# A diffusion layer on one core: probabilities transposed through DRAM, partial sums seeded in PSUM, Newton rounds on GpSimd

## The chip, the core and the metric

The kernel runs on one core of a Trainium2 chip. A core has TensorE (PE, which loads weights and streams the moving operand past them), VectorE (DVE), ScalarE (ACT), GpSimd (POOL), and SyncE (SP), whose queue issues the DMA transfers of this kernel. PE writes to PSUM, a small memory of eight banks of 512 float32 columns; DVE, ACT and PE read SBUF, the large one. Each engine works through its own list of instructions in order and waits on semaphores for the others. The metric is device time in microseconds (us), as the median of several executions.

## The reference, cut to what matters

One layer over 256 latent tokens and 256 context tokens of width 2048, all in float32.

```python
sh1, sc1, g1, sh2, sc2, g2 = ada_mods(c, w_ada, b_ada)             # modulation of the latents
qa, ka, va, qb, kb, vb = mixer_qkv(modulate(x, sh1, sc1), w_in, ...)   # B: per-head rms norm of q, k; rotary
qac, kac, vac, qbc, kbc, vbc = mixer_qkv(modulate(ctx, csh1, csc1), w_in, ...)
heads = concatenate([window_sink_attention(qa, ka, va, kac, vac, sink_logit),
                     global_attention(qb, kb, vb, kbc, vbc)], axis=-1)
x = layer_norm(DN_ALPHA * x + g1 * (heads @ w_out), ln1_g, ln1_b)
x = layer_norm(DN_ALPHA * x + g2 * swiglu(modulate(x, sh2, sc2), w_gate, w_up, w_down), ln2_g, ln2_b)
```

There are 16 query heads of 128, eight in group A (windowed, with a sink) and eight in group B (global), each group with two key heads. A query attends in one softmax to 256 latent and 256 context keys, so a row of scores has 512 entries. For the product of probabilities and values the probabilities must lie with the keys on the partitions, while the softmax has the queries there: that is the transpose of which this change speaks.

## The kernel before, in words

Every weight product is done as three float32r products of split operands (`mm3`, lines 268 to 271): high by high, low by high, high by low. So a weight tile is loaded by SP (a "raw" buffer of 1 MB), its high part is cast by ACT and its low part subtracted by DVE (lines 491 and 494 in the first part, 259 and 260 in the second), and only then can PE use it.

The first part, up to about 406 us, is recorded as steps and put in order by a planner, `Flow`. Each step has an engine, a cost in ns, the steps it waits for, and the buffers that it takes and gives; a step can ask for its result to count as ready earlier or later than its end. `Flow.forward` plays the steps against the clock with these costs and lags (the lag after a step on SP is 2000 ns), `Flow.backward` gives each its latest start, and the best of eight rounds is the order in which the instructions are issued. So the planner's costs decide the order on each engine, and nothing is reordered on the chip.

In that part the layer's input is modulated and the combined projection is accumulated over five groups of input columns (`GROUPS`, with 1, 1, 2, 4 and 8 tiles of 128): `flow_block` makes the products of a group for one block of 512 output columns, and after each group the sum in PSUM is added on DVE to `qacc` or `kvacc` in SBUF (line 679). `head_rms` computes the reciprocal root for the norms of group B's heads: squares on ACT, then a first guess and three Newton rounds on small tiles of DVE (lines 288 to 290, 720). `flow_keys` and `flow_queries` rotate, transpose and split keys and queries.

`flow_attend` does the attention in 16 pairs of heads (four head groups of four heads, two blocks of 128 queries). For a pair: scores on PE, the largest on DVE (L873), exponentials on ACT (L885), the reciprocal on DVE (L895), the weighting on ACT (L898); then, for each of the two heads, four transposes on PE into a PSUM bank (L903) and a copy to SBUF by ACT (L908, `gather`); then the product with the values on PE (L914), a cast on ACT (L921) and a subtraction on DVE (L925). Pools set how many can be under way: `b4` has 18 tiles of 4 KB a partition, `t2k` five of 2 KB, `wk` and `acc` four PSUM banks each.

`flow_out` makes the output projection. It is done in pieces over the four head groups: a first piece is copied to `outacc` by ACT (L1080); a later one is added on DVE (L1086); the last is then gated (L1089), joined with the residual (L1092, L1095) and measured for the layer norm (L1098). While the attention runs, SP also brings `w_out` and the rest of `w_ada`, of which DVE makes the gate's sums (L377).

The second part, from about 406 us on, is the feed-forward network, in an order set by its loops and not by `Flow`. It already transposes its hidden activations by way of DRAM: `squares` (DVE transposes 32 by 32 blocks, L1367), `put` (four DMAs, one for each 32 partitions, L1372) and `get` (one DMA back, L1377).

Of the kernel before, what the change touches and what calls it, by code (L numbers as in the profile page):

```python
# [22 lines left out]
P = 128  # L23
# [30 lines left out]
PUT, GET, PLACE = 6, 8, 9  # L54

# [139 lines left out]
def dit_layer(ctx: ExitStack, tc: tile.TileContext, x, c, cx, c_ctx, w_ada, b_ada, w_in, q_norm_g,  # L195
# [72 lines left out]
    def mm3(ps, xh, xl, w, first, last):  # L268
        nc.tensor.matmul(ps, lhsT=xh, rhs=w[0], start=first, stop=False)  # L269
        nc.tensor.matmul(ps, lhsT=xh, rhs=w[1], start=False, stop=False)  # L270
        nc.tensor.matmul(ps, lhsT=xl, rhs=w[0], start=False, stop=last)  # L271

    def rsqrt_steps(ss, n, done):
# [12 lines left out]
        def newton(i):  # L286
            y, t = st["y"], st["t"]
            nc.vector.scalar_tensor_tensor(t, y, -0.5, y, op0=ALU.mult, op1=ALU.mult)
            nc.vector.tensor_mul(t, t, ss())
            nc.vector.scalar_tensor_tensor(y, t, 1.5, y, op0=ALU.add, op1=ALU.mult)  # L290
            if i == 2:
                done(y)

        return [first] + [lambda i=i: newton(i) for i in range(3)]

    ea = ExitStack()
# [203 lines left out]

    def flow_products(hl, deps, ready, cols, ps, xs, first, last, prev):

        def fn():
            if first:
                ps.t = acc_bank()
            for i, (c, x) in enumerate(zip(cols, xs)):
                xh, xl = x()
                mm3(ps.t, xh, xl, (hl.hi[:, c : c + NB], hl.lo[:, c : c + NB]),
                    first and i == 0, last and i == len(cols) - 1)
# [3 lines left out]
        return F.add("PE", 681 * len(cols), fn, after, [ps] if first else [], list(hl.rooms))  # L513
# [132 lines left out]
    def flow_block(g, b, chunks):  # L646
# [7 lines left out]
        ends = {}  # L654
# [19 lines left out]
        for r in rows:  # L674
            dst = qacc[gi][r] if kvi is None else kvacc[kvi][r // 2][:, r % 2, :]

            def evac(dst=dst, ps=accs[r], r=r):
                if g > 0:
                    nc.vector.tensor_add(dst, dst, ps.t)
                elif r % 2 or b < 2:  # L680
                    nc.vector.tensor_copy(dst, ps.t)
                else:
                    nc.scalar.copy(dst, ps.t)

            eng = "ACT" if g == 0 and not (r % 2 or b < 2) else "DVE"
            evacs[b, r] = F.add(eng, 520 if eng == "ACT" else 710, evac, [ends[r], evacs.get((b, r))], give=[accs[r]])
# [19 lines left out]
    def head_rms(srcs, nh, after, scale=None):  # L706
# [10 lines left out]
        def done(y):  # L717
            if scale is not None:
                f = pa.tile([P, n], F32, tag="qsc", name="qsc", bufs=4)
                nc.vector.tensor_scalar_mul(f, y, scale)  # L720
# [4 lines left out]
        for i in range(len(srcs)):  # L725
            for h in range(nh):
                squares.append(F.add("ACT", 440, lambda i=i, h=h: square(i, h), [*after, *squares[:1]]))
        prev = squares
        for f in rsqrt_steps(lambda: st["ss"], n, done):
            prev = [F.add("DVE", 720, f, prev)]  # L730
# [18 lines left out]
    def flow_keys(w):  # L749
# [10 lines left out]
        for r in range(4):  # L760
# [34 lines left out]
            else:  # L795
                a = F.add("DVE", 1360 * (r < 2) + 800 * w, turn, [ev[r], root, tables], [rot] if r < 2 else [])
            a = F.add("PE", 210, flip, [a], [ps], [rot] if r < 2 else [])
            a = F.add("ACT", 300, cast, [a, *kT[w][1][:1]], rooms if r == 0 else [])
            b = F.add("DVE", 420, rest, [a], give=[ps])
# [4 lines left out]
    def flow_queries(gi):  # L804
# [8 lines left out]
        for t in range(NT):  # L813
# [25 lines left out]
            for i, ns in enumerate((420, 420, 710, 710)):  # L839
# [3 lines left out]
            a = F.add("ACT", 500, cast, [a, *(c for c, _ in qT[gi][1])], rooms if t == 0 else [])  # L843
            b = F.add("DVE", 710, rest, [a], give=[ps])
            qT[gi][1].append((a, b))

    def flow_attend(gi, at, each):
# [5 lines left out]
        for p in range(4):  # L853
# [4 lines left out]
            pT, o_ps = Buf("b4"), Buf("wk")  # L858
# [41 lines left out]
            def flip(i, probs=probs, ps=None):  # L900
                ps.t = wk_bank()
                for k in range(4):
                    nc.tensor.transpose(ps.t[:, k * P : (k + 1) * P], probs[i].t[:, k * P : (k + 1) * P], ident)  # L903

            def gather(i, pT=pT, ps=None):
                if i == 0:
                    pT.t = b4([P, 4, 2, P], F32, "pT")
                nc.scalar.copy(pT.t[:, :, i, :], ps.t.rearrange("p (k q) -> p k q", k=4))  # L908

            def values(pT=pT, o_ps=o_ps):  # L910
                o_ps.t = wk_bank()
                for k in range(4):
# [296 lines left out]
    at = TO  # L1209
# [410 lines left out]
```

## Time and profile before

| What | Value |
|---|---|
| Median of three runs | 1156.96 us (1155.35 to 1157.27) |
| The profiled execution's own time | 1156.38 us |
| Its span, from the first to the last instruction | 1154.6 us |
| Mean granted TensorE clock | 0.996 |
| HBM read, written | 295.68 MB, 7.86 MB |
| Wait of PE for `crow`, the longest of all | 3.0 us |
| End of the last matmul, start of the closing layer norm | 1133 us |

How to read the profile's rows: a group's row has the source line, the engine, the operation, the tiles (out<-in), the shape and the count, then the busy time in us, the mean ns of one, and behind the second bar the idle time of the engine just before the group, with what ended it. A row of the waits has the engine and line that waited, what it waited for, then total us, number and longest. A row of the windows has a stretch of the span, its length, each engine's busy time in it (with the count of instructions), the granted clock, the share of the DMA engines and GB/s. A row of the timeline or of the chain starts with the start in us and the duration.

### The profile page before, as it was taken

To read this page: it belongs to the slowest core of one execution; us is meant where nothing else is said; L and a number is where in the kernel's file an instruction comes from. 1 tells how busy PE (TensorE), PEld (TensorE's weight loads), DVE (VectorE), ACT (ScalarE), POOL (GpSimd) and SP (SyncE) were. 2 spreads that over 40 slices of the span, in tenths; PEclk is the share of its full clock that TensorE was granted. 3 is DMA by queue.
4 is the path that set the end of the run, shared out by engine and by line. 5 is a ranking of instruction groups with operands and counts; after the bars stand their busy time and mean duration, and the time that the engine had idled before them with its cause. 6 is when DMAs were issued, how large, how long until landed. Compare 5 with 4: busy or idle time off the path is not lost.

```text
span 1154.6 us, 14326 instructions
## 1 busy us (share of the span) xinstructions
PE 1135.0 (98%) x5475; PEld 919.1 (80%) x5475; DVE 830.9 (72%) x1078; ACT 540.2 (47%) x772; POOL 26.1 (2%) x44
## 2 busy tenths in 40 slices
PE   8999999999999999999999999999999999999995
PEld 8766588888888768888888888888888888888884
DVE  4763489988899988777666666776776787676556
ACT  3331442678776255544464444544544344433341
POOL 1000030000000001000000000000000000000000
PEclk9999999999999999999999999999999999999998
DMA  8999998624588578989967776677677988876641
GB/s 263 382 381 394 396 363 311 221 74 160 185 316 296 175 250 309 349 305 317 312 196 258 224 244 223 225 248 250 227 247 248 323 308 301 315 292 236 208 142 74
DMA packets 166557, 304.49 MB, mean 264 GB/s; under 512 B 7340, under 2 KB 33356, under 8 KB 164183
## 3 DMA queue, kind: packets, MB, share of 16 engines
q1 hardware_dynamic: 166488, 303.58, 75.7%
q8 instruction: 43, 0.70, 0.2%
q14 instruction: 26, 0.21, 0.1%
HBM read 295.68 MB, written 7.86 MB: 263 GB/s over the span
## 4 chain that ended last, share of the span: by engine, by line
PE 94%; DVE 2%; DMA 2%; ACT 1%; issue 0%; SPq 0%; DVEq 0%; ACTq 0%
PE acc L269 27%; PE acc L270 27%; PE acc L271 27%; PE wk L914 2%; PE wk L530 2%; PE acc L1124 1%; PE wk L903 1%; DMA raw<-in_w_in_dram 1%; PE wk L269 1%; PE wk L271 1%; PE wk L270 1%; PE wk L387 1%; PE wk L617 1%; DMA lgb<-in_ln_b_dram 1%; PE wk L967 0%
## 5 line engine op out<-in xcount | busy, mean ns | idle before, releaser
L260 DVE TENSOR_TENSOR lo<-raw,hi 128x1024 fp32r<-128x1024 f32 x258 | 312.5, 1220 | 182.8 <-ACT hi L259 179.3
L259 ACT CAST hi<-raw 128x1024 fp32r<-128x1024 f32 x258 | 271.2, 1055 | 353.4 <-PE acc L271 306.5
L269 PE MATMUL acc<-hi,u2h 128*128 128x512 f32 x704 | 274.6, 390 | 0.2 <-ACT u2h L1443 0.2
L270 PE MATMUL acc<-lo,u2h 128*128 128x512 f32 x704 | 274.0, 389 | 0.7 <-DVE lo L260 0.7
L271 PE MATMUL acc<-hi,u2l 128*128 128x512 f32 x704 | 274.1, 389 | 0.0
L269 PEld LDWEIGHTS acc<-hi,u2h 128*128 128x128 f32 x704 | 132.2, 188 | 28.2 <-ACT u2h L1443 1.1
L270 PEld LDWEIGHTS acc<-lo,u2h 128*128 128x128 f32 x704 | 132.2, 188 | 28.2 <-DVE lo L260 1.1
L271 PEld LDWEIGHTS acc<-hi,u2l 128*128 128x128 f32 x704 | 132.2, 188 | 28.2 <-DVE u2l L1444 0.6
L491 ACT CAST hi<-raw 128x1024 fp32r<-128x1024 f32 (+1 forms) x86 | 87.9, 1033 | 127.2 <-PE acc L271 64.4
L269 PE MATMUL acc<-hi,hTh 128*128 128x512 f32 x344 | 135.5, 394 | 0.0
L271 PE MATMUL acc<-hi,hTl 128*128 128x512 f32 x344 | 133.9, 389 | 0.0
L270 PE MATMUL acc<-lo,hTh 128*128 128x512 f32 x344 | 133.9, 389 | 0.0
L377 DVE SCALAR_TENSOR_TENSOR adav<-raw,cs,adav 128x512 f32<-128x512 f32 (+1 forms) x128 | 121.2, 947 | 9.1 <-DMA raw<-in_w_ada_dram 7.4
L494 DVE TENSOR_TENSOR lo<-raw,hi 128x1024 fp32r<-128x1024 f32 (+1 forms) x86 | 101.8, 1195 | 27.2 <-ACT hi L491 27.0
L269 PE MATMUL acc<-hi,uh 128*128 128x512 f32 x256 | 103.9, 406 | 0.1
L270 PE MATMUL acc<-lo,uh 128*128 128x512 f32 x256 | 100.3, 392 | 0.8 <-DVE lo L494 0.8
L271 PE MATMUL acc<-hi,ul 128*128 128x512 f32 x256 | 100.0, 391 | 0.0
L270 PEld LDWEIGHTS acc<-lo,hTh 128*128 128x128 f32 x344 | 64.6, 188 | 14.4 <-issue 1.0
L269 PEld LDWEIGHTS acc<-hi,hTh 128*128 128x128 f32 x344 | 64.6, 188 | 14.1 <-issue 1.0
L271 PEld LDWEIGHTS acc<-hi,hTl 128*128 128x128 f32 x344 | 64.6, 188 | 13.4
L269 PEld LDWEIGHTS acc<-hi,uh 128*128 128x128 f32 x256 | 48.1, 188 | 15.8 <-issue 5.2
L270 PEld LDWEIGHTS acc<-lo,uh 128*128 128x128 f32 x256 | 48.2, 188 | 10.5 <-DVE lo L494 1.8
(206 smaller groups left out, 1167.5 us busy)
## 6 DMA issues: line engine op xcount, KB each, us to landing
raw<-in_w_ada_dram SPq DMA_DIRECT2D x72, 1024.0 KB, 7.3
raw<-in_w_gate_dram SPq DMA_DIRECT2D x44, 1024.0 KB, 7.3
raw<-in_w_up_dram SPq DMA_DIRECT2D x44, 1024.0 KB, 7.3
raw<-in_w_down_dram SPq DMA_DIRECT2D x44, 1024.0 KB, 5.2
raw<-in_w_ada_dram SPq DMA_DIRECT2D x48, 512.0 KB, 4.5
raw<-in_w_in_dram SPq DMA_DIRECT2D x18, 1024.0 KB, 9.9
raw<-in_w_out_dram SPq DMA_DIRECT2D x16, 1024.0 KB, 5.0
raw<-in_w_in_dram SPq DMA_DIRECT2D x10, 512.0 KB, 6.9
```

What stands on the lines that cost most here:

```text
L259: nc.scalar.copy(hi[:, :n], raw[:, s : s + n])
L260: nc.vector.tensor_tensor(lo[:, :n], raw[:, s : s + n], hi[:, :n].bitcast(F32), op=ALU.subtract)
L269: nc.tensor.matmul(ps, lhsT=xh, rhs=w[0], start=first, stop=False)
L270: nc.tensor.matmul(ps, lhsT=xh, rhs=w[1], start=False, stop=False)
L271: nc.tensor.matmul(ps, lhsT=xl, rhs=w[0], start=False, stop=last)
L377: nc.vector.scalar_tensor_tensor(a[:, c : c + piece], raw[:, f : f + piece], cs[:, 4 * (g * (G4 * NB // w) + j) + 2, None], a[:, c : c + p ...
L387: nc.tensor.matmul(ps, lhsT=ones, rhs=sb[:, s : s + NB], start=True, stop=True)
L491: nc.scalar.copy(hl.hi[:, :n], raw.t[:, s : s + n])
L494: nc.vector.tensor_tensor(hl.lo[:, :n], raw.t[:, s : s + n], hl.hi[:, :n].bitcast(F32), op=ALU.subtract)
L530: nc.tensor.matmul(bank.t[32 * j : 32 * j + 32, :width], lhsT=cs[:, 4 * k + 2 - 2 * i : 4 * k + 34 - 2 * i], rhs=raw.t[:, c * width : (c + ...
L617: nc.tensor.transpose(ps.t[:, (j * 2 + t) * P : (j * 2 + t + 1) * P], src, ident)
L914: nc.tensor.matmul(o_ps.t[:, : 2 * P], lhsT=v, rhs=pT.t[:, k].rearrange("p h q -> p (h q)"), start=k == 0, stop=k == 3)
```

## The change

It has three parts, and new costs for the planner.

First, `flow_attend` no longer transposes on PE. DVE transposes each head's probabilities in squares of 32 by 32 into a tile `hx` (4 KB a partition, from `b4`) that holds both heads; four DMAs write it to a DRAM tile of 512 KB (`put`), and one DMA reads it back as `pT` (`get`), with key positions on the partitions. The columns of `pT` are then ordered by block of 32 queries first and head second, so the product with the values reads its moving operand with the pattern `pv[:, k]` (8 runs of 32), and the cast and the subtraction behind it put the result back in order. The planner gets the extra steps with their lags: `LANDING` adds 4500 ns to the time between a `put` and its `get`, 2500 ns to that between the `get` and the values.

Second, sums go on in PSUM. For the last of the five groups (`SEED_G = 4`) and for the later pieces of the output projection, ACT copies the sum so far from SBUF into the PSUM bank (`flow_seed`), the products accumulate on it, and ACT copies the result back where it is kept. The adds on DVE go; the end of the output projection is gate, residual and measure for all four column blocks alike.

Third, the three Newton rounds and the scaling in `head_rms` go from DVE to GpSimd, as four simpler instructions a round. The warm-up products at the start use a `wk` bank in place of an `acc` bank.

```diff
+SEED_G = 4
+LANDING = 4500, 2500
...
         def newton(i):
             y, t = st["y"], st["t"]
-            nc.vector.scalar_tensor_tensor(t, y, -0.5, y, op0=ALU.mult, op1=ALU.mult)
-            nc.vector.tensor_mul(t, t, ss())
-            nc.vector.scalar_tensor_tensor(y, t, 1.5, y, op0=ALU.add, op1=ALU.mult)
+            nc.gpsimd.tensor_mul(t, y, y)
+            nc.gpsimd.tensor_mul(t, t, ss())
+            nc.gpsimd.tensor_scalar(t, t, -0.5, 1.5, op0=ALU.mult, op1=ALU.add)
+            nc.gpsimd.tensor_mul(y, y, t)
...
+    def flow_seed(ps, src, after):
+        def fn():
+            ps.t, ps.seeded = acc_bank(), True
+            nc.scalar.copy(ps.t, src())
+        return F.add("ACT", 475, fn, after, [ps])
...
         rows = range(2 if kvi is None else 4)
         accs = [Buf("acc") for r in rows]
-        ends = {}
+        sums = [qacc[gi][r] if kvi is None else kvacc[kvi][r // 2][:, r % 2, :] for r in rows]
+        ends = {r: flow_seed(accs[r], lambda r=r: sums[r], [evacs[b, r], chunks[0][0][1][0]]) for r in rows} if g >= SEED_G else {}
...
+            def evac(dst=sums[r], ps=accs[r], eng=eng):
+                if eng == "ACT":
+                    nc.scalar.copy(dst, ps.t)
+                elif g > 0:
                     nc.vector.tensor_add(dst, dst, ps.t)
...
-            def flip(i, probs=probs, ps=None):
-                ps.t = wk_bank()
-                for k in range(4):
-                    nc.tensor.transpose(ps.t[:, k * P : (k + 1) * P], probs[i].t[:, k * P : (k + 1) * P], ident)
-
-            def gather(i, pT=pT, ps=None):
-                if i == 0:
-                    pT.t = b4([P, 4, 2, P], F32, "pT")
-                nc.scalar.copy(pT.t[:, :, i, :], ps.t.rearrange("p (k q) -> p k q", k=4))
+            def squares(i, probs=probs, hx=hx):
+                if i == 0:
+                    hx.t = b4([P, 4, 2, P], F32, "hx")
+                nc.vector.transpose(hx.t[:, :, i, :].rearrange("p r (k q) -> p k r q", k=4),
+                                    probs[i].t.rearrange("p (k r q) -> p k r q", r=4, k=4))
+
+            def put(hx=hx, st=st):
+                st["hd"] = scratch.tile([4, 32, 4, 2 * P], F32, tag="pd", name="pd", bufs=8)
+                for a in range(4):
+                    nc.sync.dma_start(st["hd"][:, :, a, :].rearrange("r i x -> i r x"),
+                                      hx.t[32 * a : 32 * a + 32].rearrange("i r h x -> i r (h x)"))
+
+            def get(pT=pT, st=st):
+                pT.t = b4([P, 4, 2, P], F32, "pT")
+                nc.sync.dma_start(pT.t.rearrange("p a h x -> p (a h x)"), st["hd"].rearrange("r i a x -> (r i) (a x)"))
...
+                pv = pT.t.rearrange("p a h (k q) -> p k (a h) q", k=4)
...
-                    nc.tensor.matmul(o_ps.t[:, : 2 * P], lhsT=v, rhs=pT.t[:, k].rearrange("p h q -> p (h q)"),
+                    nc.tensor.matmul(o_ps.t[:, : 2 * P].rearrange("p (g q) -> p g q", q=32), lhsT=v, rhs=pv[:, k],
                                      start=k == 0, stop=k == 3)
...
-                ps = Buf("wk")
-                a = F.add("PE", 390, lambda i=i, f=flip, ps=ps: f(i, ps=ps), [n[i]], [ps], [probs[i]])
-                g.append(F.add("ACT", 520, lambda i=i, f=gather, ps=ps: f(i, ps=ps), [a, *g], [pT] if i == 0 else [], [ps]))
+                g.append(F.add("DVE", 615, lambda i=i, f=squares: f(i), [n[i], *g], [hx] if i == 0 else [], [probs[i]]))
+            a = F.add("SP", 2000, put, g, give=[hx])
+            g = [(F.add("SP", 1300, get, [(a, -LANDING[0])], [pT]), -LANDING[1])]
...
-            if gs[-1] < 3:
-                outs[n, t] = steps([ends[t], outs[n, t]], add, give=[ps])
-            elif by_tile:
...
+            if gs[-1] < 3:
+                outs[n, t] = F.add("ACT", 475, copy, [ends[t], ropes[n, t]], give=[ps])
+                return
+            a = F.add("DVE", 710, gate, [ends[t], gates[n]], give=[ps])
+            a = F.add("DVE", 710, base, [(a, 80)])
+            outs[n, t] = F.add("DVE", 710, spread, [(a, 80)])
```

Besides, several costs that the planner works with are lowered (for example 440 to 300 ns for a square on ACT, 420 to 350 ns and 710 to 615 ns for subtractions and adds on DVE), and the order of the whole first part is planned anew with them.

More of the change, by code (lines that the diff above doesn't have):

```diff
@@ L842, in flow_queries @@
             a = F.add("PE", 400, flip, [a], [ps], [rot])
-            a = F.add("ACT", 500, cast, [a, *(c for c, _ in qT[gi][1])], rooms if t == 0 else [])
-            b = F.add("DVE", 710, rest, [a], give=[ps])
+            a = F.add("ACT", 475, cast, [a, *(c for c, _ in qT[gi][1])], rooms if t == 0 else [])
+            b = F.add("DVE", 615, rest, [a], give=[ps])
             qT[gi][1].append((a, b))
@@ L1048, in flow_out @@
         F.at = at
-        ends = {}
+        first = pieces[0][2][1][0]
+        ends = {t: flow_seed(accs[t], lambda t=t: outacc[n, t], [outs[n, t], first]) for t in range(NT)} if gs[0] else {}
         def products(gi, i, piece, t):
@@ L1126, in dit_layer @@
     nc.vector.tensor_copy(identb, ident)
[L1127 removed]
+    wps = Buf("wk")
     def warm_step(i):
         if i == 0:
[L1131 removed]
+            wps.t = wk_bank()[:, :P]
         warm(wps.t, 1)
```

94 lines of the change are left out of this document (35 added, 59 removed).

## The prediction

> **What bounds the kernel now.** I read the page's engine table first, then the engine's waits, then the windows by stage.
>
> ```profile
> span 1154.6 us, 14326 instructions
> PE 1135.0 (98%) x5475; PEld 919.1 (80%) x5475; DVE 830.9 (72%) x1078; ACT 540.2 (47%) x772; POOL 26.1 (2%) x44
> PE acc L269 27%; PE acc L270 27%; PE acc L271 27%; PE wk L914 2%; PE wk L530 2%; PE acc L1124 1%; PE wk L903 1%; DMA raw<-in_w_in_dram 1%; PE wk L269 1%; PE wk L271 1%; PE wk L270 1%; PE wk L387 1%; PE wk L617 1%; DMA lgb<-in_ln_b_dram 1%; PE wk L967 0%
> 206.00:363.00 157.00, 157.00 (x792) 128.94 (x791) 138.41 (x259) 119.39 (x260) 0.00 (x0) 1.00 0.58 201
> 363.00:406.00 43.00, 43.00 (x204) 32.87 (x202) 40.74 (x63) 12.81 (x15) 1.77 (x4) 1.00 0.59 199
> 360.00:380.00 20.00, 20.00 (x83) 15.24 (x82) 19.82 (x23) 9.71 (x13) 0.00 (x0) 1.00 0.92 306
> 50.00:100.00 50.00, 50.00 (x277) 33.84 (x276) 29.62 (x41) 17.42 (x26) 0.00 (x0) 1.00 1.02 382
> ```
>
> The first two lines: TensorE (PE) is busy for 1135.0 of 1154.6 us. The third is the chain that ended last, by line: nearly all PE, and L903, the transposes of the probabilities, is in it with 1%. The other four are stages (start and end, length, then busy us of PE, PEld, DVE, ACT and POOL, the granted clock, the share of the DMA engines, GB/s). The attention runs from 206 to 363 us, the last output products to 406. In both PE is busy in every microsecond at clock 1.00; DVE has 157.00 - 138.41 = 18.6 us and 2.3 us idle, 20.9 together, and the DMA engines work 0.58 of the time. So a microsecond taken off PE between 206 and 406 comes off the end, as long as DVE and the transfers keep up.
>
> **Part 1: the transposes leave PE.** The chain in order of time gives what they cost there, better than their durations, which overlap:
>
> ```profile
> 223.00 0.44 PE wk L903 x4
> 223.44 0.23 PE acc L269
> ...
> 227.44 1.78 PE wk L914 x8
> ```
>
> Four transposes hold PE for 0.44 us. There are 16 pairs of heads with two groups each: 32 x 0.44 = 14.1 us less. The products with the values (L914, 1.78 us a pair) stay, but read their moving operand as 8 runs of 32 elements, not as 256 in a row. The trace shows no such read on PE. On DVE it costs nothing:
>
> ```profile
> L739 DVE TENSOR_TENSOR qrot<-qacc,sinQ 128x256 f32<-128x256 f32 x4 | 1.7, 414 | 0.0
> L744 DVE TENSOR_TENSOR krot<-krot,kvacc 128x256 f32<-128x256 f32 x4 | 1.7, 424 | 0.1
> ```
>
> L739 reads runs of 32, L744 whole rows: 414 against 424 ns. I take 0; the upper end, a doubled time, is 16 x 1.78 = 28.5 us. A gain is excluded, since the columns stay.
>
> **Part 2: what DVE, ACT and GpSimd do instead.** Rows of DVE between 206 and 406 us, then of the whole run:
>
> ```profile
> L679 DVE TENSOR_TENSOR qacc<-qacc,acc 128x512 f32<-128x512 f32 x6 | 4.1, 680 | 0.6 <-PE acc L271 0.6
> L679 DVE TENSOR_TENSOR kvacc<-kvacc,acc 128x512 f32<-128x512 f32 x1 | 0.7, 677 | 0.0
> L1086 DVE TENSOR_TENSOR oacc<-oacc,acc 128x512 f32<-128x512 f32 x8 | 5.4, 679 | 0.3 <-PE acc L271 0.2
> L1095 DVE TENSOR_TENSOR xt<-xt,oacc 128x512 f32<-128x512 f32 x2 | 1.4, 692 | 0.1
> L1089 DVE TENSOR_TENSOR oacc<-acc,g1b 128x512 f32<-128x512 f32 x2 | 1.4, 692 | 0.7 <-PE acc L271 0.7
> L288 DVE SCALAR_TENSOR_TENSOR rs_t<-rs_y 128x8 f32<-128x8 f32 x9 | 1.4, 156 | 0.0
> L289 DVE TENSOR_TENSOR rs_t<-rs_t,ss 128x8 f32<-128x8 f32 x9 | 1.5, 168 | 0.3
> L290 DVE SCALAR_TENSOR_TENSOR rs_y<-rs_t,rs_y 128x8 f32<-128x8 f32 x9 | 1.5, 167 | 0.3
> L720 DVE TENSOR_SCALAR qsc<-rs_y 128x8 f32<-128x8 f32 x2 | 0.3, 171 | 0.1
> L1367 DVE STREAM_TRANSPOSE spill<-spill 128x512 f32<-128x512 f32 x20 | 13.0, 685 | 0.0
> L908 ACT COPY pT<-wk 128x512 f32<-128x512 f32 x32 | 18.5, 595 | 4.4 <-PE wk L903 4.0
> ```
>
> DVE gets 32 transposes in squares: 32 x 0.685 = 21.9 us. It loses the adds of the last group that lie in the stage (4.1 + 0.7), those of the output sums (5.4 + 1.4 + 1.4) and the Newton rounds (1.4 + 1.5 + 1.5 + 0.3): 17.7 us. Net +4.2: 138.4 + 40.7 + 4.2 = 183.3 us of work in 200 - 14.1 = 185.9. Of its 20.9 us of rest, 2.6 are left. Lower bound of the loss: none, if DVE can run that densely; between 360 and 380 us it was busy for 19.82 of 20.00, 0.9% idle. Upper bound: it keeps today's share of rest, 20.9 / 200 = 10.4%, and needs 183.3 / 0.896 = 204.6 us, 18.7 more than there are. Near the dense row, at 2.5% idle, it needs 188.0: I take 2.1 us lost.
>
> ACT loses 32 gathers (18.5 us) and gets 16 + 10 seeds and 16 + 2 copies, 44 x 0.595 = 26.2 us, part of it ahead of 206; it is busy for 119.4 of 157 and takes +7.7. A seed is issued before the product it starts, so PE waits for it only where ACT is behind; without that cover each costs 0.595. I take 0. Start flags and the warm-up's other bank cost PE nothing: the same instructions.
>
> GpSimd gets three sets of 12 small instructions and two scalings, 38. The nearest rows, a part of GpSimd's and DVE's timeline:
>
> ```profile
> 445.70 1.23 DVE L260 TENSOR_TENSOR lo<-raw,hi 128x1024 fp32r<-128x1024 f32 x1 [0.61 <-ACT hi L259]
> 445.87 1.12 POOL L960 TENSOR_TENSOR mA<-lcol,sc 128x4 f32<-128x4 f32 x1
> 446.85 1.28 DVE L377 SCALAR_TENSOR_TENSOR adav<-raw,cs,adav 128x1024 f32<-128x1024 f32 x1
> 446.94 1.24 POOL L961 TENSOR_TENSOR mB<-lcol,sc 128x4 f32<-128x4 f32 x1
> 448.26 0.20 POOL L962 TENSOR_TENSOR mB<-mB,sh 128x4 f32<-128x4 f32 x1
> 256.86 0.17 DVE L720 TENSOR_SCALAR qsc<-rs_y 128x8 f32<-128x8 f32 x1
> 292.82 0.15 DVE L881 SCALAR_TENSOR_TENSOR nm<-m,qsc 128x2 f32<-128x2 f32 x1
> ```
>
> The operation takes 0.20 us alone and 1.12 to 1.24 beside a DVE instruction. A set of 12 lasts 2.4 to 14.9 us instead of DVE's 9 x 0.16 = 1.5. What hides it: a query's scale was ready at 256.86 (L720) and first read at 292.82 (L881), 36 us later. Cost 0; without that cover, up to 13.4 us a set. The Trainium skill (SBUF — State Buffer, section "SBUF: two separate sides") says that VectorE and GpSimd take turns at one pair of ports, held for a whole instruction. The 1.12 beside 1.23 us agrees for GpSimd; that DVE too is held off would speak against the change, and is a rival below.
>
> **Part 3: the way through DRAM.** Transfers of before that do the same with smaller pieces (instructions' rows, then the landings of L1372 and of L1377, then issues):
>
> ```profile
> L1372 SPq DMA_DIRECT2D hd<-spill x80: 303/450/663, 640.0 to 862.0; - x80
> DMA to landing us min/median/max: 1.6/4.4/7.1
> DMA to landing us min/median/max: 5.2/5.3/5.5
> raw<-in_w_out_dram SPq DMA_DIRECT2D x16, 1024.0 KB, 5.0
> SPq L469 <- DVE lo L494: 100.7, 16, 19.0
> ```
>
> A pair adds two squares (1.4 us), four puts (4 x 0.45 to issue, the last landing 1.6 to 7.1 us after), and one get (0.4 to issue, 5.2 to 5.5): 1.4 + 1.8 + 4.4 + 0.4 + 5.3 = 13.3 us where a flip and a gather took 0.44 + 0.595 each. PE covers it only by products placed in between. The planner's constants allow 2.0 + 4.5 us from a put's start to its get and 1.3 + 2.0 + 2.5 from there to the values, 12.3 together; the rows give 1.8 + 4.4 + 0.4 + 5.3 = 11.9, so a median transfer is in time. A slow put (7.1) is 2.7 - 0.4 = 2.3 us late. If every second pair's delay also covers the next (pairs stand 157/16 = 9.8 us apart, less than the 12.3), all late would be 8 x 2.3 = 18 us, half of them 9. I take 0, by the median. Traffic: 16 x (0.5 + 0.5) MB = 16.8 MB at the 382 GB/s of 50 to 100 us is 44 us; with 0.58 x 157 = 91 that makes 135 of 143 us. The queue is nearly full too. In SP's queue the puts wait for the squares and the gets for the puts; behind them wait the loads of w_out and w_ada, and for those the casts on ACT and then PE. Against harm: between 200 and 400 us SP waited 100.7 us for free buffers already (the last row), and in the changed queue 14 of the 16 gets have a load or another pair's puts between them and their own puts.
>
> **Sum.** -14.1 (transposes) + 2.1 (DVE) = -12.0 on the profiled execution's 1156.4 us, of which the span is 1154.6: 1144.4. The median of the three runs, 1156.96, is 0.6 above the profiled one: **1145.0 us**. What could come on top is the one wait that PE has at the stage's end:
>
> ```profile
> L1294 PE MATMUL wk<-ident,xt 128*128 128x128 f32 x8 | 1.3, 283 | 1.4 <-DVE xt L1040 1.4
> ```
>
> I leave it in; without it and with no DVE loss the time is 1141.5.
>
> **Rivals.**
> - *DVE becomes the bound, and it is slower.* Place: the stage from 206 to 406. At today's rest of 10.4% the loss is 18.7, 4.6 more than the gain: 1161.6 us. It decides from 16.7 us of needed rest on (9%). For it: the 2.6 us that are left. Against: 0.9% rest between 360 and 380. Chance 0.08.
> - *Landings are late by the slow put*, half of the pairs: 1145.0 + 9 = 1154.0, a little faster. For: 7.1 in the row. Against: the median. 0.10.
> - *GpSimd holds DVE off*: 38 instructions of at least 0.20 us are 7.6 us, beyond the 2.1 taken 5.5 more: 1150.5. Against: L377 above took 1.28 us beside L961, what it takes anyway. 0.07.
> - *SP's queue runs dry*: while SP waits for a landing of 4.4 us, the put's own 0.5 MB takes 1.4, so the queue idles for 3.0; 16 times that is 48, of which 143 - 135 = 8 are free: 40 late, 1185. Against: the 14 of 16. 0.05.
> - *The broken read doubles the values' products*: 1145.0 + 28.5 = 1173.5. 0.03.
> - The forecast: 0.67.
>
> **How the numbers follow.** The forecast's own range is 1140 (no DVE loss, no wait at L1294, and the 1.6 us by which the fastest of the three runs lies below the median) to 1148. Adding the GpSimd and the landing case, the range 1139.5 to 1154 holds about 0.8; the bounds of 18.7 and 28.5 us lie above it with their small chances. 0.2% is 2.3 us, about what a measurement can tell here: faster means below 1154.6. That is 0.67 + 0.07 + 0.07 of the landing case + 0.02 of a milder DVE case = 0.83; same 0.05; slower 0.12.
>
> **What would show it.** Right: no L903 rows; PE idle in the stage under 3 us, its waits named DVE lo and not DMA pT; the L914 group still 1.7 us a pair; the first output flip near 394 us instead of 406; DVE over 97% busy in the stage; HBM writes of 16.2 MB instead of 7.86; DMA share near 0.9. Wrong: PE waiting for pT from DMA at the values (late landings), for lo from DVE over 10 us (DVE the bound), raw buffers late behind the gets (SP), values' products longer than 380 ns each (the broken read), or DVE instructions longer beside GpSimd's.

## The result, and the profile after

The changed kernel takes 1141.26 us (median of four runs, 1140.97 to 1141.57) against 1156.45 us (1155.35 to 1157.27) of the kernel before: a ratio of 0.9869, 95% interval 0.9852 to 0.9886, or 15.2 us less. The prediction was 1145.0 us, faster. What the rest of this document asks is why the gain came whole, though one of its terms should have eaten 2.1 us, and which part of the change it belongs to.

First the engine table of the page and its line on HBM:

```profile
span 1139.7 us, 14229 instructions
PE 1119.6 (98%) x5347; PEld 905.9 (79%) x5347; DVE 828.2 (73%) x1053; ACT 546.7 (48%) x784; POOL 42.2 (4%) x82
HBM read 304.07 MB, written 16.25 MB: 281 GB/s over the span
```

PE is busy for 15.4 us less (1135.0 to 1119.6) and has 128 instructions fewer, which are the transposes. The span is 14.9 us shorter. The DMA engines write 8.4 MB more and read 8.4 MB more.

Where on the time line the gain lies is seen at the last output product (`acc<-hi,oTl`), with which PE ends the attention and the output projection, and at the first transposes for the feed-forward network's input (L1294, now L1300). The rows in the timeline of PE, before and then after (start, duration, and in brackets the wait):

```profile
403.05 0.39 PE L271 MATMUL acc<-hi,oTl 128*128 128x512 f32 x1
403.37 2.78 PE L1261 MATMUL wk<-raw,cs 128*32 128x512 f32 x24
406.08 0.66 PE L1294 MATMUL wk<-ident,xt 128*128 128x128 f32 x4
413.67 0.63 PE L1294 MATMUL wk<-ident,xt 128*128 128x128 f32 x4 [1.36 <-DVE xt L1040]
```

```profile
389.99 0.39 PE L273 MATMUL acc<-hi,oTl 128*128 128x512 f32 x1
390.22 0.60 PE L1300 MATMUL wk<-ident,xt 128*128 128x128 f32 x4
390.75 3.64 PE L1267 MATMUL wk<-raw,cs 128*32 128x512 f32 x32
398.55 0.60 PE L1300 MATMUL wk<-ident,xt 128*128 128x128 f32 x4
```

The last output product starts 13.1 us earlier. The first transposes start 15.9 us earlier, but they are no even mark: 24 small products for `w_ada` (L1261, 2.7 us) stood ahead of them before, and now all 32 stand behind them. The second transposes no longer wait. From the last output product to the end of the span it is 1154.6 - 403.1 = 751.5 us before and 1139.7 - 390.0 = 749.7 after. So 13.1 us of the gain are made in the stage, and 1.8 behind it, where the wait of 1.4 us is gone. (The 1133 us given earlier for the end of the last matmul is where the chain of waits leaves PE; in that same trace the last matmul starts at 1141.0.) The stage in the windows, before and after (busy us of PE, PEld, DVE, ACT, POOL, then clock, DMA share, GB/s):

```profile
206.00:390.00 184.00, 184.00 (x912) 150.34 (x911) 164.46 (x293) 130.09 (x272) 1.24 (x3) 1.00 0.62 212
```

```profile
206.00:390.00 184.00, 182.96 (x838) 148.30 (x837) 172.15 (x292) 126.34 (x262) 13.88 (x38) 1.00 0.84 294
206.00:349.00 143.00, 142.46 (x652) 114.72 (x650) 133.62 (x239) 110.45 (x243) 13.88 (x38) 1.00 0.83 286
```

PE stays full: 1.0 us idle in 184. DVE rises from 164.5 to 172.2 us, which leaves it 11.8 us. The waits of PE over the whole run, longest first:

```profile
PE wk L316 <- DMA crow<-in_c_ctx_dram: 3.0, 1, 3.0
PE acc L272 <- DVE lo L498: 1.5, 2, 0.8
PE acc L273 <- DVE oTl L951: 1.0, 2, 0.9
PE acc L272 <- DVE lo L262: 0.8, 1, 0.8
```

No row names `pT`: the way through DRAM never holds PE up. The wait for `oTl` is the one in the stage. The two `lo` rows stood at 0.8 and 0.7 us before. The groups of instructions that the prediction priced, and then the two kinds of transfer (rows of the instructions, then the landings of tile `pd`, the put, and of tile `pT`, the get; the trace tells the landing of 8 of the 64 puts and of one of the 16 gets, which is why that one's three values are equal):

```profile
L939 PE MATMUL wk<-pT,kvacc 128*128 128x256 f32 x128 | 30.1, 379 | 0.0
L921 DVE STREAM_TRANSPOSE hx<-pr 128x512 f32<-128x512 f32 x32 | 22.3, 701 | 0.9 <-ACT pr L914 0.9
L291 POOL TENSOR_TENSOR rs_t<-rs_t,ss 128x8 f32<-128x8 f32 x9 | 3.7, 411 | 0.7
L293 POOL TENSOR_TENSOR rs_y<-rs_y,rs_t 128x8 f32<-128x8 f32 x9 | 1.9, 208 | 0.8
```

```profile
L927 SPq DMA_DIRECT2D pd<-hx x64: 302/432/1103, 222.4 to 345.7; - x64
DMA to landing us min/median/max: 2.3/4.2/6.3
L932 SPq DMA_DIRECT2D pT<-pd x16: 337/344/702, 230.5 to 350.7; - x16
DMA to landing us min/median/max: 6.3/6.3/6.3
```

### The profile page after: what moved, and what is told of

It reads as the page before. It is cut to its first block, busy times and chain, and to the rows that moved or that the text cites. A ratio compares the mean times of both kernels' runs of the same rounds, so it can differ in the third digit from the quotient of the medians.

```text
span 1139.7 us, 14229 instructions
## 1 busy us (share of the span) xinstructions
PE 1119.6 (98%) x5347; PEld 905.9 (79%) x5347; DVE 828.2 (73%) x1053; ACT 546.7 (48%) x784; POOL 42.2 (4%) x82
## 3 DMA queue, kind: packets, MB, share of 16 engines
HBM read 304.07 MB, written 16.25 MB: 281 GB/s over the span
## 4 chain that ended last, share of the span: by engine, by line
PE 90%; DMA 5%; DVE 3%; ACT 1%; issue 0%; POOL 0%; SPq 0%; DVEq 0%; POOLq 0%; ACTq 0%
PE acc L271 27%; PE acc L273 27%; PE acc L272 27%; DMA raw<-in_w_ada_dram 2%; PE wk L546 2%; PE wk L939 2%; PE wk L1130 1%; DMA raw<-in_w_in_dram 1%; DMA raw<-in_w_out_dram 1%; DMA pd<-hx 1%; PE wk L271 1%; PE wk L273 1%; PE wk L272 1%; PE wk L633 1%; PE wk L992 0%; DVE lo L498 0%
## 5 line engine op out<-in xcount | busy, mean ns | idle before, releaser
L381 DVE SCALAR_TENSOR_TENSOR adav<-raw,cs,adav 128x512 f32<-128x512 f32 (+1 forms) x128 | 121.3, 948 | 13.4 <-DMA raw<-in_w_ada_dram 11.2
L272 PEld LDWEIGHTS acc<-lo,uh 128*128 128x128 f32 x256 | 48.1, 188 | 11.8 <-DVE lo L498 2.6
```

Source lines behind the costliest of these rows:

```text
L381: nc.vector.scalar_tensor_tensor(a[:, c : c + piece], raw[:, f : f + piece], cs[:, 4 * (g * (G4 * NB // w) + j) + 2, None], a[:, c : c + p ...
```

## The experiments

Twelve kernels were run, each timed in three rounds beside the kernel before. This table holds them all. "Change" is the median less that of the kernel before in the same series (1156.80 for t_only, no_t, newton_dve and no_seed; 1156.21 for no_t_plan2, the two thin ones and landing_short; 1156.20 for the rest), and the text compares runs by it. PE and DVE are busy us in the stretch from 206 to 390 us. The last two columns are the start of the last output product and the time from there to the end of the span; like PE and DVE they are of the one profiled execution.

| Run | Median us | Change | Ratio to before (95%) | PE | DVE | Last output product at | From it to the end |
|---|---|---|---|---|---|---|---|
| before | 1156.45 | 0 | 1 | 184.0 | 164.5 | 403.1 | 751.5 |
| after | 1141.26 | -15.2 | 0.9869 (0.9852 to 0.9886) | 183.0 | 172.2 | 390.0 | 749.7 |
| t_only | 1162.11 | +5.3 | 1.0044 (1.003 to 1.0058) | 176.4 | 173.2 | 399.7 | 762.3 |
| no_t | 1160.24 | +3.4 | 1.0028 (1.0018 to 1.0038) | 183.3 | 148.0 | 409.2 | 749.4 |
| no_t_plan2 | 1156.26 | +0.1 | 1.0005 (0.9995 to 1.0016) | 183.9 | 151.4 | 402.8 | 750.1 |
| costs_only | 1159.89 | +3.7 | 1.003 (1.0019 to 1.0041) | 184.0 | 166.8 | 402.6 | 753.3 |
| newton_dve | 1144.82 | -12.0 | 0.99 (0.9883 to 0.9916) | 182.4 | 174.0 | 392.9 | 749.6 |
| no_seed | 1158.83 | +2.0 | 1.0011 (1.0001 to 1.002) | 178.0 | 174.7 | 395.4 | 762.5 |
| no_seed_thin_same | 1154.54 | -1.7 | 0.9994 (0.9979 to 1.001) | 178.2 | 169.9 | 393.6 | 759.0 |
| no_seed_thin | 1149.67 | -6.5 | 0.9941 (0.9926 to 0.9956) | 181.3 | 174.5 | 393.1 | 754.0 |
| landing_short | 1151.65 | -4.6 | 0.9955 (0.9938 to 0.9972) | 173.1 | 160.3 | 402.6 | 748.9 |
| landing_long | 1148.00 | -8.2 | 0.9926 (0.991 to 0.9941) | 179.7 | 166.5 | 397.3 | 750.7 |
| twice | 1150.86 | -5.3 | 0.9958 (0.9942 to 0.9974) | 174.7 | 163.6 | 399.7 | 749.4 |
| q_dram | 1152.22 | -4.0 | 0.9965 (0.9951 to 0.9978) | 176.8 | 172.6 | 397.6 | 755.4 |

### One part of the change at a time

**t_only**: the transposes go through DRAM, but the sums stay with DVE and so do the Newton rounds.

```diff
-SEED_G = 4
+SEED_G = 9
...
-            nc.gpsimd.tensor_mul(t, t, ss())
+            nc.vector.tensor_mul(t, t, ss())
...
-            prev = [F.add("POOL" if i else "DVE", 1300 if i else 720, f, prev)]
+            prev = [F.add("DVE", 720, f, prev)]
...
-        ends = {t: flow_seed(accs[t], lambda t=t: outacc[n, t], [outs[n, t], first]) for t in range(NT)} if gs[0] else {}
+        ends = {}
```

> Only the way through DRAM (with its planner lags and the new step costs); sums are added on DVE and Newton's rounds stay on DVE, as before. My theory (PE is the bound, but its 14.1 us only come off while DVE has room, and the seeds and GpSimd make that room): DVE needs 179.2 + 21.9 = 201 us in the stages from 206 us to the first output flip, against 186 that PE would leave, so DVE becomes the bound and the time is about that of before, 1151 to 1162 us. Rival (the transposes alone bring it all, DVE finds room elsewhere): 1141 to 1145.

1162.11 us, 5.3 more than before and at the upper end of what was expected: with 14.1 us taken off PE the kernel is slower. The window of the stage, and the longest waits that PE has:

```profile
206.00:390.00 184.00, 176.40 (x783) 139.41 (x783) 173.17 (x315) 112.69 (x238) 0.00 (x0) 0.99 0.81 280
```

```profile
PE acc L273 <- DVE u2l L1467: 3.2, 1, 3.2
PE wk L938 <- ACT pr L900: 3.2, 2, 2.3
PE acc L272 <- DVE lo L497: 2.5, 5, 0.8
```

DVE is no busier than in the changed kernel (173.2 against 172.2 us), but it has more to do: the work that does not fit comes later. PE now has 7.6 us idle in the stage, of which 4.2 are waits that name DVE and 3.2 name ACT (`pr`). From the last output product to the end it takes 762.3 us, 12.6 more than in the changed kernel; the wait of 3.2 us for DVE's `u2l` and a low clock behind it lie there.

**no_t**: the other way round, seeds and GpSimd rounds, with the transposes back on PE and ACT (the removed `flip` and `gather` of the change's diff).

```diff
-                g.append(F.add("DVE", 615, lambda i=i, f=squares: f(i), [n[i], *g], [hx] if i == 0 else [], [probs[i]]))
-            a = F.add("SP", 2000, put, g, give=[hx])
-            g = [(F.add("SP", 1300, get, [(a, -LANDING[0])], [pT]), -LANDING[1])]
+                ps = Buf("wk")
+                a = F.add("PE", 390, lambda i=i, f=flip, ps=ps: f(i, ps=ps), [n[i]], [ps], [probs[i]])
+                g.append(F.add("ACT", 520, lambda i=i, f=gather, ps=ps: f(i, ps=ps), [a, *g], [pT] if i == 0 else [], [ps]))
```

> Seeds and Newton's rounds on GpSimd as in the changed kernel, but the probabilities are transposed on PE and gathered by ACT as before. My theory: PE keeps its 14.1 us, so 1154 to 1157, at best the 1.4 us wait at the first output flip less. Rival (DVE's relief or the new planner costs bring part of the gain by themselves): 1148 or less.

1160.24 us, 3.4 more than before and above the expected 1154 to 1157. DVE falls to 148.0 us in the stage and PE is full there, so the relief of DVE buys nothing by itself. That the kernel gets slower has another place, which PE's timeline shows, with the windows around it:

```profile
129.69 0.80 PE L271 MATMUL acc<-hi,uh 128*128 128x512 f32 x1 [2.85 <-ACT hi L495]
...
131.97 0.63 PE L271 MATMUL acc<-hi,uh 128*128 128x512 f32 x1
132.40 0.63 PE L272 MATMUL acc<-lo,uh 128*128 128x512 f32 x1
```

```profile
130.00:136.00 6.00, 5.53 (x13) 3.99 (x13) 3.86 (x4) 3.09 (x4) 0.00 (x0) 0.50 1.04 385
136.00:142.00 6.00, 6.00 (x35) 3.49 (x34) 2.42 (x3) 0.69 (x1) 0.00 (x0) 0.98 0.78 266
```

A cast on ACT comes late in this order, far ahead of the attention; PE waits 2.85 us and then gets half its clock for 6 us.

**no_t_plan2** is the same kernel with the planner's cost for a seed raised, which gives another order.

```diff
-        return F.add("ACT", 475, fn, after, [ps])
+        return F.add("ACT", 520, fn, after, [ps])
```

> As no_t (PE transposes, seeds, Newton's rounds on GpSimd), with a seed planned at 520 in place of 475 ns; this gives another order, in which the product that waited 2.8 us at 127 us for its cast has its weights earlier. My theory (seeds and GpSimd bring nothing while PE keeps the transposes, and no_t lost 5 us to that early wait and the low clock behind it): 1153.5 to 1157, clock 1.00 between 120 and 140 us. Rival (the seeds themselves cost): 1159 and more.

1156.26 us, ratio 1.0005: the time of before. The wait at 129 us is 0.2 us long here and the clock stays at 1.00. So no_t's loss goes with that wait and its clock, and seeds and GpSimd rounds without the new transposes bring nothing.

**costs_only**: the kernel before with the changed costs of the planner and the warm-up's other bank, every operation where it was.

```diff
-                squares.append(F.add("ACT", 440, lambda i=i, h=h: square(i, h), [*after, *squares[:1]]))
+                squares.append(F.add("ACT", 300, lambda i=i, h=h: square(i, h), [*after, *squares[:1]]))
...
-            m = [F.add("DVE", 700, lambda i=i, f=largest: f(i), [s[i]]) for i in range(2)]
+            m = [F.add("DVE", 615, lambda i=i, f=largest: f(i), [s[i]]) for i in range(2)]
```

> The kernel before with only the planner's new costs (reductions 0.615, rotations 1.2, squares 0.3, sums 0.615 and so on) and the warm-up's other bank; every operation stays where it was: PE transposes the probabilities, DVE adds all sums and does the Newton rounds. Theory (PE is full either way, 184.0 of 184 us between 206 and 390, so a better plan has nothing to close): 1153 to 1160 us, within 0.3% of before. Rival (a part of the 15 us is the plan's own): 1151 us or less.

1159.89 us, ratio 1.003. The first theory's band holds the time, the bound of 0.3% that it names is just reached, and the rival is out. The new costs alone give an order that is no better for the old operations; PE is busy in all 184.00 us of the stage, as before.

### How much DVE can bear

**newton_dve**: the changed kernel with only the Newton rounds back on DVE.

```diff
-            nc.gpsimd.tensor_mul(t, y, y)
-            nc.gpsimd.tensor_mul(t, t, ss())
-            nc.gpsimd.tensor_scalar(t, t, -0.5, 1.5, op0=ALU.mult, op1=ALU.add)
-            nc.gpsimd.tensor_mul(y, y, t)
+            nc.vector.scalar_tensor_tensor(t, y, -0.5, y, op0=ALU.mult, op1=ALU.mult)
+            nc.vector.tensor_mul(t, t, ss())
+            nc.vector.scalar_tensor_tensor(y, t, 1.5, y, op0=ALU.add, op1=ALU.mult)
```

> The changed kernel with Newton's rounds and the scaling back on DVE. My theory: DVE gets 4.7 us back, 179 of 186 us in the stage, still room: 1141 to 1143.5. Rival (GpSimd's instructions hold DVE off, 38 of them at 0.2 to 0.4 us, 7 to 15 us): faster than the changed kernel by 2 us or more, 1139 or less. Other rival (DVE has no room left): 1146 and more.

1144.82 us: 12.0 less than before, 3.2 short of the changed kernel, and between the bands of the theory and of the other rival. If GpSimd's small instructions held DVE off, taking them away would have helped; it did not. The kernel is slower with 4.7 us of work put back on DVE (the four rows of L288 to L290 and L720 in the prediction), but its trace does not lay that on DVE: in the stage PE waits for DVE 0.4 us in all (`kTl`), less than the 1.0 us of the changed kernel, and over the run PE is not idle longer but busy longer (1122.3 against 1119.6 us) with the same products. The order was planned anew here as well, and what cost the 3.2 us is not shown.

**no_seed**: the changed kernel with DVE's adds back (`SEED_G = 9`, no seeds in `flow_out`, its old end with a gate ahead of the last add); Newton stays on GpSimd.

```diff
-SEED_G = 4
+SEED_G = 9
...
+            def add():
+                nc.vector.tensor_add(outacc[n, t], outacc[n, t], ps.t)
```

> The changed kernel with the sums added on DVE as before and no seeds. My theory: DVE gets 13.0 us of adds back, 187 us of work in 186: it is the bound, with PE waiting for lo and oTl from DVE, 1147 to 1155. Rival (seeds only move work between engines that have time): 1141 to 1143.

1158.83 us, 2.0 more than before and above the expected 1147 to 1155: 17.2 of gain are lost. DVE gets 24 adds of 0.68 us (16.3 us) and two more at the end. The longest wait of PE in the stage, the stage's window, and the place where the rest shows up:

```profile
PE wk L939 <- DVE kTl L804: 2.3, 2, 1.3
206.00:390.00 184.00, 178.04 (x808) 143.19 (x806) 174.65 (x292) 112.98 (x238) 15.94 (x38) 1.00 0.87 298
395.00:410.00 15.00, 9.83 (x64) 5.87 (x63) 14.51 (x34) 4.39 (x9) 1.70 (x4) 0.86 0.60 217
```

DVE is at 174.7 of 184 in the stage, and all of PE's 6.0 idle us there are waits that name DVE (`kTl` 2.3, `oTl` 1.9, `lo` 0.9, `qTl` 0.5, `qrot` 0.4). Behind it DVE is at 14.5 of 15, where PE is down to 9.8 of 15, at clock 0.86 (the same wait for `u2l` as in t_only lies there, 2.4 us).

To part DVE's time from the order that comes with it, **no_seed_thin_same** keeps the order of no_seed and makes those 24 adds short: they cover one column of 512, so all other columns of 24 partial sums are left out. **no_seed_thin** has the same short adds, and the planner is told of them. (The edit, against no_seed.)

```diff
-                    nc.vector.tensor_add(dst, dst, ps.t)
+                    m = 1 if g == 4 else NB
+                    nc.vector.tensor_add(dst[:, :m], dst[:, :m], ps.t[:, :m])
...
-                nc.vector.tensor_add(outacc[n, t], outacc[n, t], ps.t)
+                nc.vector.tensor_add(outacc[n, t][:, :1], outacc[n, t][:, :1], ps.t[:, :1])
```

> As no_seed, in the same order of instructions, but the 24 adds of sums (16 after the last group, 8 in the output) touch one column of 512, which leaves those partial sums out of the result. DVE does about 24 x 0.55 = 13 us less. If DVE's time alone was what made no_seed slow (1158.8 us): 1144 to 1149. If it was the order, with DVE's adds standing in its queue where they wait for the end of PE's products and with steps planned around them: 1153 and more.

> The same thin adds, with their cost lowered to 130 ns for the planner, so that the order is made for them. DVE's load is then within about 6 us of the changed kernel's. My theory (DVE's time in this stage decides, and the planner must know of it): 1142 to 1148. Rival (an add on DVE costs by its place in the queue, whatever its length): 1153 and more.

1154.54 and 1149.67 us. The first lies in the band that was named for the order, the second between its two bands: neither fell where the load alone would have put it. Shortening the adds in an order made for long ones returns 3.7 of the 17.2 us; planning for the short ones returns 8.5. The other 8.7 are not the length of these adds. In no_seed_thin PE waits 2.5 us for `xt` at the second transposes for the feed-forward network's input, at the old end of the output projection, which no_seed and its two variants share; the rest of the 8.7 is not assigned.

**q_dram**: the changed kernel with the queries' transposes sent through DRAM as well, a further trade of PE's time for DVE's and the queue's.

```diff
-            a = F.add("PE", 400, flip, [a], [ps], [rot])
-            a = F.add("ACT", 475, cast, [a, *(c for c, _ in qT[gi][1])], rooms if t == 0 else [])
+            a = F.add("DVE", 615, blocks, [a], [hx], [rot])
+            a = F.add("SP", 2000, put, [a], give=[hx])
+            a = F.add("SP", 700, get, [(a, -LANDING[0])], [qp])
+            a = F.add("ACT", 530, cast, [(a, -LANDING[1]), *(c for c, _ in qT[gi][1])], rooms if t == 0 else [])
```

> The changed kernel with the queries' transposes (16 tiles of four squares, L843 of the changed kernel's queries) sent the same way through DRAM: PE loses 16 x 0.44 = 7.0 us, DVE gets 16 x 0.70 = 11.2 us more, 8.4 MB more traffic. Theory (DVE at 172 of 184 us is close to all that this order can use, so a trade of PE time for more DVE time has come to its end): no faster than the changed kernel, 1141 to 1152 us, and PE's waits name DVE (lo, oTl). Rival (PE alone is the bound, DVE has 10 us left): 1134 to 1138 us.

1152.22 us, 4.0 less than before and just above the expected 1141 to 1152. (There are 8 such tiles and not 16: PE has 32 transposes fewer, 3.5 us, DVE 5.6 us more.) PE gets 3.5 us less to do and 11.2 us of the gain are lost: further trade does not pay here. The waits of PE in the stage, longest first, and the part of it in which the two longest single waits lie (at 283.3 and 311.9 us):

```profile
PE wk L955 <- DMA pT<-pd: 2.2, 2, 1.7
PE wk L273 <- DVE qTl L863: 1.7, 1, 1.7
```

```profile
280.00:320.00 40.00, 35.84 (x157) 29.03 (x157) 34.43 (x55) 22.82 (x42) 6.44 (x13) 1.00 0.97 338
```

Against the expectation the longest of them is for a landing. In that part DVE is busy for 34.4 of 40 us and the DMA engines' share is 0.97, so this run does not show DVE's limit apart from the queue's.

### The way through DRAM

**landing_short** and **landing_long** are the changed kernel with other lags in the plan; the operations are the same.

```diff
-LANDING = 4500, 2500
+LANDING = 500, 500
```

```diff
-LANDING = 4500, 2500
+LANDING = 9000, 6000
```

> The changed kernel with LANDING = 500, 500: the planner takes a get to be possible 2.5 us after the put's end and the values 2.5 + 1.3 us after the get. The landings of the changed kernel were 2.3 to 6.3 us. My theory (the long ways are needed): PE waits for pT from DMA at several of the 16 pairs, 1146 to 1158. Rival (there is slack enough in the order anyway): 1141 to 1144.

> The changed kernel with the planner's two lags doubled (9.0 us from a put to its get instead of 4.5, 6.0 instead of 2.5 to the values). Theory (the measured landings of at most 6.3 us are covered by the lags as they are, so more lag buys nothing and only keeps tiles longer): 1141 to 1146 us, PE's waits for pT none, as in the changed kernel. Rival (the lags as they are still cost something that no wait names): 1139 us or less.

1151.65 and 1148.00 us: both lose part of the gain, 10.6 and 7.0 us. With short lags, PE's waits:

```profile
PE wk L939 <- DMA pT<-pd: 3.4, 2, 2.7
PE wk L939 <- ACT pr L914: 2.9, 1, 2.9
PE acc L271 <- ACT acc L510: 2.6, 1, 2.6
```

The get's landing (median 5.2 us of the four that the trace tells) is no longer covered at two pairs. Besides, PE waits for probabilities (`pr`) and for a seed (`acc<-` by ACT) in this order: 10.9 us of PE idle in the stage, of which 3.4 are for landings. With long lags no row names `pT`, as the first theory says, but its band ended at 1146: PE waits for `oTl` (2.0) and five times for `lo` (3.1 together), and 4.3 us are idle in the stage. More lag was not free in this order; whether the lag costs that or the order that happened to come with it, these runs do not tell.

**twice** writes every pair's tile a second time, into a tile that nothing reads. It is one more DMA of 512 KB for each of the 16 pairs, and not the 64 more of which the expectation speaks; the bytes are the same.

```diff
+                idle = scratch.tile([4, 32, 4, 2 * P], F32, tag="pe", name="pe", bufs=8)
...
+                nc.sync.dma_start(idle.rearrange("r i a x -> (r i) (a x)"), hx.t.rearrange("p r h x -> p (r h x)"))
```

> Every put of the probabilities is issued a second time, into DRAM tiles that nothing reads: 64 more DMAs (64 x 0.43 = 28 us of issue on SP's queue) and 8.4 MB more written. The transfers are at 0.83 of 143 us in the changed kernel, so about 24 us of the engines' time are free; 8.4 MB at the 382 GB/s of 50 to 100 us are 22. Theory (the changed kernel has just enough room in the queue, and uses less than the 135 of 143 us that the prediction worked out): 1141 to 1149 us, HBM writes 24.6 MB. Rival (the queue is already what the order leans on, as the prediction's sum of 135 of 143 would have it): the loads behind the puts come late, 1151 us or more, and PE's waits name casts (hi, lo) behind a raw from DMA.

1150.86 us, 9.9 of the gain lost, between the two bands and next to the rival's; but the waits are not the ones that the rival names. PE's waits in the stage (those for `pT` lie between 295 and 331 us), its last part, and the landings of the get:

```profile
PE wk L941 <- DMA pT<-pd: 4.5, 3, 2.2
PE acc L273 <- DVE oTl L953: 4.1, 3, 2.7
```

```profile
349.00:390.00 41.00, 36.24 (x155) 28.53 (x154) 37.84 (x43) 15.77 (x22) 0.00 (x0) 1.00 0.99 364
DMA to landing us min/median/max: 4.1/6.6/7.3
```

Of the landings that the trace tells (10 of the 64 puts), the median is 6.9 us (4.2 in the changed kernel) and the longest 10.9 (6.3). So the transposes' own way gets longer than the lags, and no wait of PE in the stage names a weight's cast. The changed kernel's queue does not take these 8.4 MB without loss.

## Why the prediction was right

- **The gain's place and size.** The term of -14.1 us is shown: no transposes of the probabilities are left on PE, and the last output product stands 13.1 us earlier, which is the 14.1 less the 1.0 us that PE waits for `oTl`. Behind the stage the one wait is gone that the prediction left in its sum, 1.4 us for `xt` (L1294). Together that is -14.5; the two profiled spans differ by 14.9 and the medians by 15.2, and the rest is small differences both ways (a row of 32 warm-up products took 4.8 us before and 3.9 after; the waits for `lo` are 0.8 us longer). The forecast gain of 12.0 was 3.2 too small: 1.1 of it is the DVE term, 1.4 that wait, and 0.7 is not assigned. That the time comes so close to the 1141.5 which the prediction gave for "without it and with no DVE loss" is in part luck, since there was a loss of 1.0.
- **The mis-sized term: +2.1 for DVE.** It came to 1.0 us, and the load behind it was far from the forecast. The prediction put 183.3 us of DVE work into 185.9 us by adding the change's balance (+4.2) to what the stage held before. Measured are 172.2 us in 184, with 11.8 us of rest. The missing 11 us are work that is no longer in the stage. The largest share is the gate's sums; in the stage, before and after, and then ahead of 206 us, before and after:

```profile
L377 DVE SCALAR_TENSOR_TENSOR g1b<-raw,cs,g1b 128x1024 f32<-128x1024 f32 x15 | 19.1, 1277 | 0.0
L377 DVE SCALAR_TENSOR_TENSOR g1b<-raw,cs,g1b 128x1024 f32<-128x1024 f32 x18 | 23.2, 1304 | 3.6 <-DMA raw<-in_w_ada_dram 3.6
L679 DVE TENSOR_TENSOR kvacc<-kvacc,acc 128x512 f32<-128x512 f32 x31 | 20.6, 682 | 18.6 <-PE acc L271 18.6
```

```profile
L381 DVE SCALAR_TENSOR_TENSOR g1b<-raw,cs,g1b 128x1024 f32<-128x1024 f32 x10 | 12.7, 1274 | 1.5 <-DMA raw<-in_w_ada_dram 1.5
L381 DVE SCALAR_TENSOR_TENSOR g1b<-raw,cs,g1b 128x1024 f32<-128x1024 f32 x22 | 28.5, 1304 | 2.1 <-DMA raw<-in_w_ada_dram 2.1
L698 DVE TENSOR_TENSOR kvacc<-kvacc,acc 128x512 f32<-128x512 f32 x24 | 15.8, 684 | 16.2 <-PE acc L273 16.1
```

  The seeds took adds off DVE ahead of 206 us too (`kvacc` 20.6 to 15.8 us, and `qacc`), and there the planner put gate sums that had been in the stage: 19.1 to 12.7 us inside, 23.2 to 28.5 ahead. The other 4.6 us are one of the eight steps at the output's end, which now lies behind the first transposes (2.1), the subtraction of one weight tile (1.7) and of two key tiles (0.8). The prediction counted the seeds "part of it ahead of 206" for ACT only, and held the rest of DVE's work fixed.
- **That the transposes need DVE's relief** is what the parts show. The transposes alone, which give DVE 22.3 us and take nothing from it, cost 5 us (t_only); relief alone gives nothing (no_t_plan2); both together give 15.2. The rival "DVE becomes the bound" thus has its place and its sign right, in t_only and no_seed, where PE's waits in the stage name DVE for 4.2 and 6.0 us. How much of their losses is DVE's time and how much the order that the planner made is not separated: of no_seed's 17.2 us, shortening the adds with the plan returned 8.5. The forecast that DVE would be over 97% busy in the stage is wrong: it is at 94%, and no run above went over 95.
- **GpSimd at nothing** is right. A set of twelve takes (3.7 + 3.7 + 3.7 + 1.9) / 3 = 4.3 us by the four groups of L290 to L293, between the bounds of 2.4 and 14.9, and PE waits for none. DVE is not held off: the gate's sums take 1274 ns against 1277, and removing the GpSimd rounds made it slower.
- **The values' broken read at nothing** is right: 379 ns each, and 1.73 us for a pair in the chain, where it was 1.73 to 1.78.
- **Landings at nothing** is right: no wait of PE names `pT`, and with short lags some do (landing_short). The puts whose landing is known are as forecast (4.2 in the median, 6.3 at most); the one known get took 6.3 us, where the two known ones that the prediction read took 5.2 and 5.5. The rival that SP's queue runs dry did not come: between 200 and 400 us SP waited 10.2 us in all for puts to land, 3.0 at most, and no wait of PE over 0.2 us names a cast on ACT.
- **The queue** was over-estimated: 0.83 of 143 us are 119, where 135 were summed. The price per byte was not at fault: 286 GB/s over 143 us are 40.9 MB, and 31.6 MB of before plus 16.8 would be 48.4. So 7.5 MB of loads moved out of that stretch, as DVE's work did. Still, twice shows that the margin is small.
- **The other signs**: HBM writes are 16.25 MB (16.2 forecast), the DMA share is 0.83 to 0.84 (near 0.9), the first transposes stand at 390.2 us (near 394), 2.7 us of which are the products that moved behind them.
- **What stays open**: how much of the gain is owed to this one order. Kernels with the same operations but other lags lose 7.0 and 10.6 us, and one constant moved no_t by 3.3 us. No kernel was run in the changed order with DVE's work alone altered. With the lags as they are the order happens to leave PE 1.0 us of idle time; nothing run here says how often a plan does that.

## What to carry to other kernels

Taking work off the engine that is the bound paid its full time here only where the engine that receives it was relieved by about as much: either half alone was worth nothing or less, and both together 15 us. When a planner orders the stage, size the receiving engine's load over the whole region that the planner may move work through, and not only over the stage as it was. Give a round trip through memory its measured landing in the plan: with the lags at that size PE never waited for it here, and with shorter and longer ones 10.6 and 7.0 us of the gain went, though what share of that the changed order alone has is not shown.

## What the runs showed of the hardware

A wait of PE can cost more than its length. In no_t PE waited 2.85 us, and in the 6 us from 130 on the granted clock was 0.50: ten products in a row came 0.43 us apart instead of 0.23, another 2.0 us. The same in t_only, around its wait of 3.2 us (windows):

```profile
405.00:410.00 5.00, 1.90 (x10) 0.79 (x6) 4.93 (x6) 2.82 (x7) 1.68 (x4) 1.00 0.88 307
410.00:413.00 3.00, 1.11 (x3) 0.92 (x4) 2.96 (x6) 0.00 (x0) 0.00 (x0) 0.53 1.04 390
413.00:416.00 3.00, 3.00 (x9) 2.32 (x8) 2.93 (x11) 0.00 (x0) 0.00 (x0) 0.50 1.01 374
419.00:422.00 3.00, 2.98 (x18) 2.28 (x17) 1.90 (x5) 2.27 (x6) 0.96 (x1) 1.00 0.34 126
```

PE idles for 5.0 of the 8 us to 413, then is busy throughout at half the clock (9 products in 3 us), and has the full clock again by 419. The Trainium skill (TensorE: Matmul & The Clock Gate, section "Part 1: The HAM clock gate (the "warmup" mystery)") has half rate after an idle window of about 3.4 us, until as long a window of work. The half rate agrees with both traces; in no_t a wait shorter than that window, 2.85 us, was followed by it, and it lasted through about 6 us in which PE worked. Nor does every such wait have it: in twice PE waited 2.71 us from 354.8 on, and the clock stayed at 1.00:

```profile
354.80:362.00 7.20, 4.49 (x21) 3.78 (x21) 6.39 (x8) 3.38 (x5) 0.00 (x0) 1.00 1.02 354
```

In landing_long a wait of 1.98 us, up to 360.9 us, was followed by 0.57 in the 4 us from 362 on. So these runs give no length of a wait from which the clock falls. The changed kernel, whose waits after the first 4 us are below 1 us each, runs its stage at 1.00.
